# Transposing attention's probabilities on VectorE with transfers, in place of TensorE, in a float32 decoder step

## The chip, the cores and the metric

One core of a Trainium2 chip runs the whole program. The metric is the device time of one execution in microseconds, the median over runs. A core has five engines that run their own instruction lists in order and wait for each other by semaphores: TensorE (PE, with its weight loads PEld), VectorE (DVE), ScalarE (ACT), GpSimd (POOL) and SyncE (SP), which here only issues transfers.

## The reference, cut to what matters

A decoder step over a prompt of 1024 tokens and eight single-token samples: one pooling layer, a shared key and value projection, one attention layer. All in float32. What the change touches is the attention of the prompt:

```python
s = einsum('...qkgd,...skd->...kgqs', q, k) * (HEAD_DIM ** -0.5)
mask = (kp <= qp) & (qp - kp < WINDOW) & (kp >= 0)      # WINDOW = 128
s = where(mask, s, NEG)
m = maximum(max(s), sink)
p = exp(s - m)
p = p / (sum(p) + exp(sink - m))
o = einsum('...kgqs,...skd->...qkgd', p, v)
...
y = (o * silu(gate)) @ w_out
```

There are 32 query heads of 64 channels, 4 key and value heads, and blocks of 128 queries, each of which sees its own and the preceding block's keys. Since the window is exactly 128, a query sees exactly 128 keys of the 256: key place r of its own block if r is not after the query, else place r of the block before.

## The kernel before

The prompt is cut into two chunks of 512 tokens (chunk 1 carries the eight samples too, 520 columns), with channels on partitions. The large projections are done as sums and differences of quarters (units), each product in three float32r passes (L784, L785, L786: high by high, high by low, low by high). They are staged in four phases (`ai`, `ao` for the pooling layer, `bi`, `bo` for attention), each in three groups of units, A (chunk 0), C (mixed) and B (chunk 1). A unit is cut into ticks: a tick is one half of a unit, 24 products of 260 columns or 12 of 512. `self.i` counts the ticks.

Everything else is hung on ticks. `self.on(t, go, rank)` calls `go` after the matmuls of tick `t`, in the order of rank; `soft` tasks (weight casts, sums) are put where a cost count of the program finds VectorE or ScalarE free. TensorE, VectorE and ScalarE keep the order of the source; the queues of SP and GpSimd are ordered by the framework's scheduler. All tiles come from 53 slots of SBUF, the longest free slot first (`self.mem.full()`); a load waits until the slot's last reader is done.

Attention is done for a pair of heads at a time (`attend(c, t, at, meet)`, called "a head" below; 16 for each chunk, and "the last five heads" are those of chunk 1 from the twelfth on). `at` is the tick of its scores, and its steps hang on it:

- `at`: `score` (L1880) on TensorE into PSUM; `select` and `largest` choose the 128 visible scores of each query and take the maximum;
- `at+2`, `at+3`: `expo`; `at+4`, `at+5`: `norm` (L1928), on ScalarE: probabilities with 128 queries on partitions, 8 blocks of 128 keys side by side (4 blocks of queries, 2 heads);
- `at+6`: `turn`, eight TensorE transposes into PSUM (L1933), so that keys come to lie on partitions; `at+7`: `keep`, ScalarE's copy to SBUF (L1941), and `mask`, VectorE's product with a triangle (L1945);
- `at+meet`: `values`, the value products (L1962) in full float32, which the profile shows as two records for each product; a tick later `gate` on VectorE.

SP issues the loads of weights (`in_wib`, `in_wob`, and stored sums such as `sbi`), of activations, and RoPE's moves between partitions (`partner`, L1703, four transfers of 32 partitions). The decode of the samples (`decode`, from tick b+79 on) issues sixteen tiny moves there (L2069).

Of the kernel before, what the change touches and what calls it, by code (L numbers as in the profile page):

```python
# [16 lines left out]
P = 128  # L17
# [20 lines left out]
K_ID, K_MP, K_J, K_RC = 0, 128, 256, 384  # L38
# [122 lines left out]
class Kern:  # L161
# [1685 lines left out]
    def attend(self, c, t, at, meet=8):  # L1847


        nc = self.nc  # L1850
        T = CHUNKS[c][1]
        cst = self.cst
        S = lambda: self.S
        x = {}
# [70 lines left out]
        def norm(n):  # L1925
            rs = x["sm"][3]
            for i in range(4 * n, 4 * n + 4):
                nc.scalar.activation(x["s3"][:, i, :], x["s3"][:, i, :], AF.Copy, scale=rs[:, i : i + 1])  # L1928

        def turn():  # L1930
            PT = self.S[:, 0, :]
            for i in range(8):
                nc.tensor.transpose(  # L1933
                    PT[:, i * P : (i + 1) * P], x["sc"][:, i * P : (i + 1) * P], cst[:, K_ID : K_ID + P]
                )
            x["s"].free()

        def keep():
            PT = self.S[:, 0, :]
            x["w"] = self.mem.full()  # L1940
            nc.scalar.copy(x["w"].a[:, :1024], PT)  # L1941

        def mask():
            x["wp"] = self.mem.full()
            nc.vector.tensor_mul(  # L1945
                x["wp"].a[:, :1024].rearrange("p (i k) -> p i k", k=P),
                x["w"].a[:, :1024].rearrange("p (i k) -> p i k", k=P),
                cst[:, None, K_MP : K_MP + P].to_broadcast([P, 8, P]),
            )

        def values():
            o = x["o"] = self.psO()
            _, V, Vd = self.K[c]
            for b in range(NB):
                bs = slice(b * P, (b + 1) * P)
                parts = ((V[b + 1], x["w"].a), (Vd[b], x["wp"].a))
                parts = parts if c or b else parts[:1]
                for n, (v, p) in enumerate(parts):
                    for j in range(2):
                        vs = slice((2 * (t // 8) + j) * HD, (2 * (t // 8) + j + 1) * HD)  # L1960
                        ms = slice((2 * b + j) * P, (2 * b + j + 1) * P)
                        nc.tensor.matmul(  # L1962
                            o[64 * j : 64 * j + 64, bs], v[:, vs], p[:, ms], start=n == 0, stop=n == len(parts) - 1
                        )
            x["w"].free()
            x["wp"].free()
# [41 lines left out]
        self.on(at + 4, total, 3)  # L2008
        self.on(at + 4, lambda: norm(0))
        self.on(at + 5, lambda: norm(1))  # L2010
        self.on(at + 6, turn, 1)
        self.on(at + 7, keep, 3)
        self.on(at + 7, mask, 5)
        self.on(at + meet, values, 3)
        if c:
            self.on(at + 8, first)
# [159 lines left out]
    def attention(self):  # L2176
        a, c, b = (self.first["bi", g] for g in "ACB")
        self.on(a, lambda: self.kv_open(0), 0)
        self.on(b, lambda: self.kv_open(1), 0)
        for n in range(4):  # L2180
            for i in range(2):
                self.attend(0, 2 * n + i, a + 22 + 16 * n + 8 * i + (3 if n == 3 and i else 0))
                self.attend(0, 8 + 2 * n + i, c + 30 + 24 * n + 12 * i, 12 if n < 3 else 8)
        for n in range(4):
            for i, t in enumerate((8 + 2 * n, 9 + 2 * n, 2 * n, 2 * n + 1)):
                self.attend(1, t, b + 20 + 16 * n + 4 * i, 8 + (4 * n + i > 10))
        self.decode(b + 79)
        for c, n, t in ((0, 2, b + 7), (0, 2, b + 17), (1, 3, b + 81), (1, 3, b + 90)):
            self.on(t, lambda c=c, n=n: [self.kvs[c].pop(0).free() for _ in range(n)], 5)
        self.on(b + 72, lambda: self.rt.free(), 5)  # L2190

# [295 lines left out]
```

## Time and profile before

| | |
|---|---|
| median of 3 runs (lowest, highest) | 2274.58 us (2272.61 to 2276.1) |
| span of the profiled execution | 2272.0 us |
| busy: PE, PEld, DVE, ACT, POOL | 2262.4, 2130.5, 1598.4, 1136.1, 197.8 us |
| attention of chunk 0 (first and last transposes) | 1138 to 1676 us |
| attention of chunk 1 (first and last transposes) | 1722 to 1969 us |
| DMA | 556.43 MB, mean 245 GB/s |

The span is from the first to the last recorded instruction; the runs' times hold what lies around it too, and the profiled execution is one of its own, 2.6 us under the runs' median. A group's row gives line, engine, operation, out<-in, its count, busy us and mean ns of one, and the idle time ahead of it with what ended it. Records of matmuls overlap, so their mean is longer than the distance between two starts.

### The profile page before, as it was taken

The numbers are of one execution on the slowest core, as the hardware profiler recorded it, in microseconds if no ns is written. First come the engines' busy times: TensorE is split into PE (matmuls) and PEld (weight loads), VectorE is DVE, ScalarE is ACT, GpSimd is POOL, SyncE is SP. The second block draws the span as 40 slices with busy tenths as digits, with TensorE's granted clock in tenths as the row PEclk, the third lists the DMA queues.
The fourth block names the chain that finished last, engine by engine and source line by source line (L and its number), as shares of the span: only waits on it lengthen the run. The fifth ranks groups of instructions, "written<-read, shape, count | busy, mean of one in ns | idle before, by whom it ended". The sixth has DMA issues, their size and how long they took to land.

```text
span 2272.0 us, 42903 instructions
## 1 busy us (share of the span) xinstructions
PE 2262.4 (100%) x17312; PEld 2130.5 (94%) x17312; DVE 1598.4 (70%) x2009; ACT 1136.1 (50%) x2372; POOL 197.8 (9%) x418
## 2 busy tenths in 40 slices
PE   9999999999999999999999999999999999999998
PEld 7889999999999899999888899999999998889998
DVE  7667746746667587685786876666566879687688
ACT  6344333343334443454576644545647678553365
POOL 0101001100100111000011010101000000111000
PEclk9999999999999999999999999999999999999999
DMA  9859757673657898888488776666754556898873
GB/s 305 314 209 350 233 213 256 227 249 117 243 184 261 276 336 291 292 304 297 153 295 301 245 244 205 230 195 220 244 169 124 177 189 224 284 356 304 301 250 132
DMA packets 190262, 556.43 MB, mean 245 GB/s; under 512 B 26096, under 2 KB 31600, under 8 KB 190064
## 3 DMA queue, kind: packets, MB, share of 16 engines
q1 hardware_dynamic: 147936, 401.82, 54.0%
q0 software_dynamic: 41984, 151.61, 17.4%
q8 instruction: 135, 2.21, 0.4%
q14 instruction: 63, 0.52, 0.1%
q10 hardware_dynamic: 144, 0.27, 0.0%
HBM read 371.88 MB, written 171.16 MB: 239 GB/s over the span
## 4 chain that ended last, share of the span: by engine, by line
PE 96%; DVE 2%; ACT 1%; DMA 0%; issue 0%; SPq 0%; ACTq 0%; DVEq 0%
PE pD L784 28%; PE pD L786 28%; PE pD L785 28%; PE pD L1351 4%; PE pO L1962 2%; PE pS L1880 2%; PE pS L1933 1%; PE pD L848 1%; DVE m L619 0%; DMA m<-in_wia 0%; DVE m L407 0%; PE pO L848 0%; DMA m<-in_x 0%; PE pO L2087 0%; DVE m L1693 0%
## 5 line engine op out<-in xcount | busy, mean ns | idle before, releaser
L784 PE MATMUL pD<-m,m 128*128 128x260 f32 (+1 forms) x4736 | 1428.6, 302 | 0.4 <-ACT m L894 0.4
L786 PE MATMUL pD<-m,m 128*128 128x260 f32 (+1 forms) x4736 | 1420.7, 300 | 0.0
L785 PE MATMUL pD<-m,m 128*128 128x260 f32 (+1 forms) x4736 | 1420.2, 300 | 0.2 <-DVE m L619 0.2
L784 PEld LDWEIGHTS pD<-m,m 128*128 128x128 f32 x4736 | 891.7, 188 | 38.8 <-issue 5.5
L786 PEld LDWEIGHTS pD<-m,m 128*128 128x128 f32 x4736 | 891.4, 188 | 32.7
L785 PEld LDWEIGHTS pD<-m,m 128*128 128x128 f32 x4736 | 891.8, 188 | 31.9 <-DVE m L619 0.6
L407 DVE TENSOR_TENSOR m<-m,m 128x1024 fp32r<-128x1024 f32 x358 | 435.1, 1218 | 144.2 <-ACT m L399 118.9
L399 ACT CAST m<-m 128x1024 fp32r<-128x1024 f32 x358 | 373.0, 1045 | 48.4 <-DVE m L443 11.7
L443 DVE TENSOR_TENSOR m<-m,m 128x1024 f32<-128x1024 f32 x200 | 243.8, 1219 | 10.4 <-DMA m<-in_woa 2.5
L915 ACT COPY m<-pD 128x260 f32<-128x260 f32 (+1 forms) x126 | 56.0, 444 | 306.4 <-PE pD L786 306.0
L619 DVE TENSOR_TENSOR m<-m,m 128x1040 fp32r<-128x1040 f32 x108 | 130.0, 1234 | 24.1 <-ACT m L613 11.8
L924 ACT ACTIVATE m<-pD 128x260 f32<-128x260 f32 x100 | 38.7, 387 | 180.8 <-PE pD L786 172.7
L926 DVE TENSOR_TENSOR m<-pD,m 128x260 f32<-128x260 f32 x100 | 42.6, 426 | 113.0 <-PE pD L786 109.8
L613 ACT CAST m<-m 128x1040 fp32r<-128x1040 f32 x108 | 111.2, 1061 | 14.6 <-DVE m L407 6.7
L1915 ACT ACTIVATE m<-m,sm 128x128 f32<-128x128 f32 x256 | 99.2, 392 | 0.0
L1351 PE MATMUL pD<-m,m 128*128 128x260 f32 (+1 forms) x576 | 91.5, 319 | 0.0
L1351 PEld LDWEIGHTS pD<-m,m 128*128 128x128 f32 x576 | 82.0, 188 | 8.3
L896 ACT COPY m<-pD 128x260 f32<-128x260 f32 x68 | 25.6, 377 | 124.9 <-PE pD L786 124.9
L1945 DVE TENSOR_TENSOR m<-m,cst 128x1024 f32<-128x1024 f32 x32 | 39.1, 1221 | 69.0 <-ACT m L1941 68.7
L1928 ACT ACTIVATE m<-m,sm 128x128 f32<-128x128 f32 x256 | 81.8, 395 | 7.1 <-DVE sm L1923 7.1
L881 ACT ACTIVATE m<-pD 128x512 f32<-128x512 f32 x50 | 29.8, 597 | 99.4 <-PE pD L786 90.6
L894 ACT ACTIVATE m<-pD 128x260 f32<-128x260 f32 x68 | 26.4, 388 | 101.3 <-PE pD L786 101.3
(246 smaller groups left out, 1857.1 us busy)
## 6 DMA issues: line engine op xcount, KB each, us to landing
m<-in_wib SPq DMA_DIRECT2D x96, 512.0 KB, 5.0
m<-in_wia SPq DMA_DIRECT2D x94, 512.0 KB, 5.6
m<-in_woa SPq DMA_DIRECT2D x48, 512.0 KB, 6.2
m<-in_wob SPq DMA_DIRECT2D x48, 512.0 KB, 7.0
sbi<-m POOLq DMA_DIRECT2D x36, 512.0 KB, 4.2
m<-sbi SPq DMA_DIRECT2D x36, 512.0 KB, 4.5
m<-in_x SPq DMA_DIRECT2D x32, 520.0 KB, 7.4
sai<-m POOLq DMA_DIRECT2D x32, 512.0 KB, 3.9
```

The source lines that it names most:

```text
L399: self.nc.scalar.copy(e["hi"].r[:, :1024], e["raw"].a[:, :1024])
L407: self.nc.vector.tensor_sub(o.r[:, :1024], s.a[:, :1024], e["hi"].a[:, :1024])
L443: self.nc.vector.tensor_add(s[o].a[:, :1024], s[a].a[:, :1024], s[b].a[:, :1024])
L613: self.nc.scalar.copy(h.r[:, : 2 * TMAX], s.a[:, : 2 * TMAX])
L619: self.nc.vector.tensor_sub(o.r[:, : 2 * TMAX], s.a[:, : 2 * TMAX], h.a[:, : 2 * TMAX])
L784: nc.tensor.matmul(ps[:, :w], wh[:, s], h, start=new and n2 == 0, stop=False, skip_group_check=on)
L785: nc.tensor.matmul(ps[:, :w], wh[:, s], l, start=False, stop=False, skip_group_check=on)
L786: nc.tensor.matmul(ps[:, :w], wl[:, s], h, start=False, stop=n2 == 7, skip_group_check=on)
L915: self.evac(ph, pos)(self.dest(ph, pos, m, 0)(cs), ps[:, : cs.stop - cs.start])
L1351: nc.tensor.matmul(ps[:, : cs.stop - cs.start], ws[:, s], d[:, cs], start=f0 and k == 0, stop=l0 and k == 3,)
L1915: nc.scalar.activation(x["s3"][:, i, :], x["s3"][:, i, :], AF.Exp, bias=nm[:, i : i + 1], scale=0.125, accum_out=rs[:, i : i + 1],)
L1928: nc.scalar.activation(x["s3"][:, i, :], x["s3"][:, i, :], AF.Copy, scale=rs[:, i : i + 1])
```

## The change

`turn` becomes one VectorE instruction: it transposes each 32x32 block of the probabilities where it stands, within its 32 partitions. A new step, `move`, then brings the blocks to the partitions on which their keys belong, by 16 transfers from SBUF to SBUF on SP's queue (32 partitions, 1 KB each). `keep` is gone. The moved tile has another order of columns (4 quarters of queries, 8 blocks, 32 queries), and `mask` and the value products read it so (`quarter`): the value product's moving operand is four runs of 32 columns. The value products come later: `meet` goes from 8 to 16 (heads 1 to 5) or 11 (heads 6 to 8) in group A of chunk 0, stays at 12 for the first six heads of group C and goes from 8 to 12 and 14 for its last two, and goes from 8 to 12 for the first eleven heads of chunk 1; the last five keep 9. `mask` stands one tick ahead of `values`. Chunk 0's keys and values are freed 5 ticks later.

```diff
         def turn():
-            PT = self.S[:, 0, :]
-            for i in range(8):
-                nc.tensor.transpose(
-                    PT[:, i * P : (i + 1) * P], x["sc"][:, i * P : (i + 1) * P], cst[:, K_ID : K_ID + P]
-                )
+            X = x["t"] = self.mem.full()
+            nc.vector.transpose(
+                X.a[:, :1024].rearrange("p (j t r) -> p t j r", j=4, t=8),
+                x["sc"][:, :1024].rearrange("p (t j r) -> p t j r", j=4, t=8),
+            )
             x["s"].free()
 
-        def keep():
-            PT = self.S[:, 0, :]
-            x["w"] = self.mem.full()
-            nc.scalar.copy(x["w"].a[:, :1024], PT)
+        def move():
+            W, X = self.mem.full(), x.pop("t")
+            x["w"] = W
+            for i in range(4):
+                for j in range(4):
+                    nc.sync.dma_start(
+                        W.a[32 * j : 32 * j + 32, 256 * i : 256 * i + 256],
+                        X.a[32 * i : 32 * i + 32, 256 * j : 256 * j + 256],
+                    )
+            X.free(True)
+
+        def quarter(a):
+            return a[:, :1024].rearrange("p (i t r) -> p i t r", i=4, t=8)
 ...
-                            o[64 * j : 64 * j + 64, bs], v[:, vs], p[:, ms], start=n == 0, stop=n == len(parts) - 1
+                            o[64 * j : 64 * j + 64, bs], v[:, vs], quarter(p)[:, :, 2 * b + j, :],
+                            start=n == 0, stop=n == len(parts) - 1,
 ...
-        self.on(at + 6, turn, 1)
-        self.on(at + 7, keep, 3)
-        self.on(at + 7, mask, 5)
+        self.on(at + 6, turn, 2)
+        self.on(at + (6 if meet < 10 else 7), move, 3)
+        self.on(at + meet - 1, mask, 5)
         self.on(at + meet, values, 3)
 ...
-                self.attend(1, t, b + 20 + 16 * n + 4 * i, 8 + (4 * n + i > 10))
+                self.attend(1, t, b + 20 + 16 * n + 4 * i, 9 if 4 * n + i > 10 else 12)
 ...
-        for c, n, t in ((0, 2, b + 7), (0, 2, b + 17), (1, 3, b + 81), (1, 3, b + 90)):
+        for c, n, t in ((0, 2, b + 7), (0, 2, b + 22), (1, 3, b + 81), (1, 3, b + 90)):
```

Where the instructions stand. On TensorE, in group B before, at the transposes of the twelfth head of chunk 1 (pS is the attention's PSUM tile, pD a projection's, m a slot):

```order
L786 MATMUL pD_20912<-m_1709_17585,m_1935_20840 128x260
L1933 MATMUL pS_11329<-cst,m_1933_20827 128x128 x8
L784 MATMUL pD_20961<-m_1702_17540,m_1929_20752 128x260
L785 MATMUL pD_20961<-m_1706_17579,m_1929_20752 128x260
L786 MATMUL pD_20961<-m_1702_17540,m_1935_20840 128x260
```

The same kind of place in the change, behind the value products of an earlier head; no row of transposes is left:

```order
L1969 MATMUL pO_21245<-m_1965_21182,m_1726_17740 64x128 x2
L1969 MATMUL pO_21245<-m_1945_20923,m_1727_17741 64x128 x2
L784 MATMUL pD_21158<-m_1700_17542,m_1938_20849 128x260
L785 MATMUL pD_21158<-m_1705_17582,m_1938_20849 128x260
L786 MATMUL pD_21158<-m_1700_17542,m_1953_21037 128x260
```

On VectorE before, around the mask of that head (L1945; L926 evacuates projections, L407 is a weight's low part, L1900 the score selection of the head after the next):

```order
L926 TENSOR_TENSOR m_1939_20910<-pD_20961,m_1921_20701 128x260
L1945 TENSOR_TENSOR m_1966_21208<-m_1965_21202,cst 128x1024
L1922 TENSOR_TENSOR sm_21097<-sm_21097,sm_21096 128x8
L1923 RECIPROCAL sm_21097<-sm_21097 128x8
L407 TENSOR_TENSOR m_1974_21265<-m_1938_20884,m_1949_21064 128x1024
L1900 COPY_PREDICATED m_1971_21255<-mki,pS_11329 128x1024
```

And in the change: the transpose (L1932), and further down the masks (L1954) of the head before and of this head, the second of which reads the moved tile m_1981:

```order
L926 TENSOR_TENSOR m_1959_21116<-pD_21118,m_1941_20887 128x260
L1932 STREAM_TRANSPOSE m_1980_21357<-m_1951_21024 128x8x4x32
...
L926 TENSOR_TENSOR m_1959_21116<-pD_21158,m_1941_20887 128x260
L1954 TENSOR_TENSOR m_1987_21426<-m_1964_21161,cst 128x1024
L1922 TENSOR_TENSOR sm_21305<-sm_21305,sm_21304 128x8
L1923 RECIPROCAL sm_21305<-sm_21305 128x8
L1954 TENSOR_TENSOR m_1995_21500<-m_1981_21360,cst 128x1024
L407 TENSOR_TENSOR m_1997_21504<-m_1955_21079,m_1989_21430 128x1024
L1900 COPY_PREDICATED m_1993_21492<-mki,pS_11329 128x1024
```

VectorE has one instruction more for each head, and its mask now waits for transfers instead of ScalarE's copy, with the next weight's low part and the next head's selection behind it. On SP's queue before, at the decode's tiny moves (L2069, in_cv the cached values):

```order
L384 DMA m_2018_21696<-in_wob 128x1024
L2063 DMA m_2016_21692<-in_cv 128x1024
L2069 DMA m_2017_21693<-m_1716_17618 1x16x8
L603 DMA m_2020_21701<-to 128x2x512
L2069 DMA m_2016_21692<-m_1716_17618 1x16x8
L603 DMA m_2022_21734<-to 128x2x512
L2069 DMA m_2016_21692<-m_1716_17618 1x16x8 x7
L2069 DMA m_2017_21693<-m_1716_17618 1x16x8 x4
```

And in the change, where the decode's moves are L2077 and a head's moves L1943 (the last head but one, then the last):

```order
L1943 DMA m_2049_21984<-m_2047_21979 32x256 x16
L384 DMA m_2052_22032<-in_wob 128x1024
L2077 DMA m_2043_21958<-m_1728_17742 1x16x8 x8
L2077 DMA m_2044_21959<-m_1728_17742 1x16x8 x4
L2080 DMA out_nvs<-m_2043_21958 128x1024
L2077 DMA m_2044_21959<-m_1728_17742 1x16x8 x4
L384 DMA m_2057_22121<-in_wob 128x1024
L1943 DMA m_2059_22138<-m_2058_22135 32x256
L2080 DMA out_nvs<-m_2044_21959 128x1024
L1943 DMA m_2059_22138<-m_2058_22135 32x256 x15
```

Sixteen issues a head are new on this queue, and between those of the last two heads stand the sixteen of the decode and four whole tiles.

More of the change, by code (lines that the diff above doesn't have):

```diff
@@ L1945, in mask @@
             nc.vector.tensor_mul(
-                x["wp"].a[:, :1024].rearrange("p (i k) -> p i k", k=P),
-                x["w"].a[:, :1024].rearrange("p (i k) -> p i k", k=P),
-                cst[:, None, K_MP : K_MP + P].to_broadcast([P, 8, P]),
+                quarter(x["wp"].a), quarter(x["w"].a),
+                cst[:, K_MP : K_MP + P].rearrange("p (i r) -> p i r", i=4)[:, :, None, :].to_broadcast([P, 4, 8, 32]),
             )
@@ L1960, in values @@
                         vs = slice((2 * (t // 8) + j) * HD, (2 * (t // 8) + j + 1) * HD)
-                        ms = slice((2 * b + j) * P, (2 * b + j + 1) * P)
                         nc.tensor.matmul(
-                            o[64 * j : 64 * j + 64, bs], v[:, vs], p[:, ms], start=n == 0, stop=n == len(parts) - 1
+                            o[64 * j : 64 * j + 64, bs], v[:, vs], quarter(p)[:, :, 2 * b + j, :],
+                            start=n == 0, stop=n == len(parts) - 1,
                         )
@@ L2179, in attention @@
         self.on(b, lambda: self.kv_open(1), 0)
[L2180 to L2183, printed above, removed]
+        at = [22, 30, 38, 46, 54, 62, 70, 81]
+        for n, (t, meet) in enumerate(zip(at, (16, 16, 16, 16, 16, 11, 11, 11))):
+            self.attend(0, n, a + t, meet)
+        for n in range(8):
+            self.attend(0, 8 + n, c + 30 + 12 * n, 12 if n < 7 else 14)
         for n in range(4):
             for i, t in enumerate((8 + 2 * n, 9 + 2 * n, 2 * n, 2 * n + 1)):
-                self.attend(1, t, b + 20 + 16 * n + 4 * i, 8 + (4 * n + i > 10))
+                self.attend(1, t, b + 20 + 16 * n + 4 * i, 9 if 4 * n + i > 10 else 12)
         self.decode(b + 79)
-        for c, n, t in ((0, 2, b + 7), (0, 2, b + 17), (1, 3, b + 81), (1, 3, b + 90)):
+        for c, n, t in ((0, 2, b + 7), (0, 2, b + 22), (1, 3, b + 81), (1, 3, b + 90)):
             self.on(t, lambda c=c, n=n: [self.kvs[c].pop(0).free() for _ in range(n)], 5)
```

## The prediction

> **What bounds the kernel now.** I read the page first: the busy shares and the chain of work that ended last.
>
> ```profile
> PE 2262.4 (100%) x17312; PEld 2130.5 (94%) x17312; DVE 1598.4 (70%) x2009; ACT 1136.1 (50%) x2372; POOL 197.8 (9%) x418
> PE 96%; DVE 2%; ACT 1%; DMA 0%; issue 0%; SPq 0%; ACTq 0%; DVEq 0%
> ```
>
> TensorE is busy all the time and is 96% of the chain: a microsecond less on TensorE is a microsecond less in all, and a microsecond in which TensorE waits is one more. Every other engine is cover. So I need two sums: what leaves TensorE, and where TensorE will now wait.
>
> **What leaves TensorE.** The groups by line (form kept apart; busy us, mean ns) and the timeline of TensorE around one batch of transposes (start, length):
>
> ```profile
> L1933 PE MATMUL pS<-cst,m 128*128 128x128 f32 x256 | 33.3, 273 | 0.0
> L1962 PE MATMUL pO<-m,m 128*64 128x128 f32 x960 | 59.5, 276 | 0.3 <-DVE m L2108 0.3
> ...
> 1299.23 0.28 PE L786 MATMUL pD<-m,m 128*128 128x260 f32 x1
> 1299.35 1.04 PE L1933 MATMUL pS<-cst,m 128*128 128x128 f32 x8
> 1300.15 0.36 PE L784 MATMUL pD<-m,m 128*128 128x260 f32 x1
> 1300.35 0.28 PE L785 MATMUL pD<-m,m 128*128 128x260 f32 x1
> 1300.47 0.28 PE L786 MATMUL pD<-m,m 128*128 128x260 f32 x1
> ```
>
> Matmul records overlap, so I price by starts. Projections start every 0.12 us. The batch takes 1299.35 to 1300.15 = 0.80, and the projection behind it waits 0.20 instead of 0.12 for its successor: 0.88 us a head. 32 heads: **-28.2 us**. The group's busy time (33.3) would count the overlap twice.
>
> The value products stay, 960 records. Their moving operand becomes four runs of 32 columns instead of one of 128. No row shows such an operand: the bounds are 0 and one more of the same, 59.5 us. I take 0: a record costs 59.5/960 = 62 ns, two (the halves j) 124 ns, in which a projection streams 260 columns, so 128 columns leave room.
>
> **What is added off TensorE.** The rows nearest to VectorE's transpose (1024 elements a partition) are these, and the second is the mask that stays:
>
> ```profile
> L1900 DVE COPY_PREDICATED m<-mki,pS 128x1024 f32<-128x1024 int32 x32 | 42.5, 1330 | 19.4 <-issue 15.4 <-ACT m L1896 3.9
> L1945 DVE TENSOR_TENSOR m<-m,cst 128x1024 f32<-128x1024 f32 x32 | 39.1, 1221 | 69.0 <-ACT m L1941 68.7 <-issue 0.3
> ```
>
> I take 1.25 us, between them (bounds 1.2 and, for an operation twice as slow, 2.5): 32 x 1.25 = 40 us more for VectorE, which is 70% busy. ScalarE loses 32 copies. Both are covered on average; where not, below. By "VectorE: DVE Perf Modes" of the Trainium skill (The three transpose paths: 311 ns for 128x128 in bf16) eight blocks would be 2.5 us, an estimate, which no run here shows; by it the sum below would be some 5 us higher.
>
> The new cost sits on SP's queue. Sixteen transfers SBUF to SBUF a head are issued one after the other. The same kind, by line: RoPE's (L1703) and the decode's (L2069), with the time from issue to landing, and eleven of them in a row:
>
> ```profile
> L1703 SPq DMA_DIRECT2D m<-m x80: 507/588/2155, 1072.0 to 1873.5; - x80
> DMA to landing us min/median/max: 2.0/4.2/8.9
> ...
> L2069 SPq DMA_DIRECT2D m<-m x16: 502/587/1566, 1940.3 to 1957.8; - x16
> DMA to landing us min/median/max: 1.7/2.9/4.6
> ...
> 1950.62 7.81 SPq L2069 DMA_DIRECT2D m<-m  x11
> ```
>
> One holds SP for 0.59 us whether it moves 128 KB or 32 bytes a partition, and about 0.64 with the step to the next; eleven took 7.81, 0.71 each. Sixteen are 16 x 0.64 = 10.2 us (11.4 by the other figure). So the path from normalized probabilities to the first value product becomes: transpose 1.25, issues 10.2, landing of the last 2.9, mask 1.22: **15.6 us** (14.7 with the shortest landing, 17 with the slow issue). The old path, transposes, copy, mask, was some 3 us.
>
> **Where the window is long enough.** The value products of chunk 0 come 5 to 10 ticks after the transpose, a tick being at least 24 x 0.12 = 2.9 us of TensorE: 14.5 us and another head's scores at the shortest. Here I put 1 us for three heads with 5 ticks. For the first eleven heads of chunk 1 a head comes every
>
> ```profile
> 1738.55 1.03 PE L1933 MATMUL pS<-cst,m 128*128 128x128 f32 x8
> 1754.66 1.03 PE L1933 MATMUL pS<-cst,m 128*128 128x128 f32 x8
> ```
>
> 16.1 us, 15.2 without its transposes. SP needs 10.2 of that, and two of RoPE's transfers and about three loads a head (some 1.3 + 1.1): 12.6, so the queue keeps up, at 83%. The window there is six ticks (17) and the products of other heads between, about 21 us: no wait. The transfers' bytes, 32 x 16 x 32 KB = 17 MB, lie in the cover of a DMA share of about a half in that stretch.
>
> **Where it is not.** The last five heads keep their value products three ticks behind the transpose. For each, the end of its normalization on ScalarE and the start of its value products on TensorE, from the timelines (start, length):
>
> ```profile
> 1897.10 1.27 ACT L1928 ACTIVATE m<-m,sm 128x128 f32<-128x128 f32 x4
> 1910.66 1.97 PE L1962 MATMUL pO<-m,m 128*64 128x128 f32 x32
> 1914.05 1.27 ACT L1928 ACTIVATE m<-m,sm 128x128 f32<-128x128 f32 x4
> 1926.88 1.31 PE L1962 MATMUL pO<-m,m 128*64 128x128 f32 x20
> 1928.68 1.29 ACT L1928 ACTIVATE m<-m,sm 128x128 f32<-128x128 f32 x4
> 1948.40 1.97 PE L1962 MATMUL pO<-m,m 128*64 128x128 f32 x32
> 1949.07 1.28 ACT L1928 ACTIVATE m<-m,sm 128x128 f32<-128x128 f32 x4
> 1963.07 1.17 PE L1962 MATMUL pO<-m,m 128*64 128x128 f32 x17 [0.29 <-DVE m L2108]
> 1966.21 1.27 ACT L1928 ACTIVATE m<-m,sm 128x128 f32<-128x128 f32 x4
> 1977.38 1.86 PE L1962 MATMUL pO<-m,m 128*64 128x128 f32 x30
> ```
>
> The windows are 12.3, 11.6, 18.4, 12.7 and 9.9 us; the head's own transposes leave them, so 11.4, 10.7, 17.5, 11.8, 9.0. Against 15.6 TensorE waits 4.2, 4.9, 0, 3.8 and 6.6. The last head has more ahead of it: in the order, all sixteen tiny transfers of the decode and four others stand between its moves and those of the head before. SP then has 1.25 + 10.2 + 16 x 0.71 + 4 x 0.35 = 24.2 us from the one normalization to the next move, and 1967.48 - 1950.35 - 0.88 + 3.8 + 1.25 = 21.3 us are there: 3 us more. Together **+22.5 us** (17 with the short landing and a turn that starts early, 32 with the slow issue). Each wait is VectorE's too: the mask that waits for the moves stands ahead of the next heads' L1900 and of weight differences (L407). That costs nothing twice, since TensorE stands still in the same time, but the stretch has no slack:
>
> ```profile
> 1900.00:1930.00 30.00, 29.92 (x226) 24.66 (x225) 29.61 (x40) 27.36 (x72) 1.75 (x4) 1.00 0.74 264
> ```
>
> The columns are the stretch, then busy time of PE, PEld, DVE, ACT and POOL, then clock, DMA share and GB/s. VectorE is busy for 29.61 of 30 us, so two transposes of 1.25 add **+2.5** (0 to 5). Loads are queued behind moves: in the order, several weights now stand only a few rows ahead of their cast. The later products also hold a head's tiles 4 to 8 ticks longer, of 53 slots that the loads need too. What waits is an engine with slack of a few us; no row prices it, the bounds are 0 and half a us for each of some twenty such loads, and I take **+3** (0 to 10).
>
> **The clock.** A wait also costs afterwards. The decode's thin matmuls are followed by a stretch at half speed:
>
> ```profile
> 1935.34 3.64 PE L2087 MATMUL pO<-qd,m 128*128 128x16 f32 x32
> ...
> 1939.15 0.46 PE L785 MATMUL pD<-m,m 128*128 128x512 f32 x1
> ...
> 1942.39 0.57 PE L784 MATMUL pD<-m,m 128*128 128x512 f32 x1
> 1942.79 0.40 PE L785 MATMUL pD<-m,m 128*128 128x512 f32 x1
> 1943.03 0.40 PE L786 MATMUL pD<-m,m 128*128 128x512 f32 x1
> ...
> 1938.80:1942.40 3.60, 3.60 (x12) 2.84 (x12) 2.08 (x6) 0.71 (x1) 0.00 (x0) 0.58 0.98 381
> ```
>
> The granted clock is 0.58 there. From 1939.15 to 1942.79, 3.64 us, nine matmuls of 512 columns start, where the last two starts shown are 0.24 apart: 9 x 0.24 = 2.2, so about 1.5 us lost, after 3.5 us of little work. I count three such losses, **+4.5** (0 to 8). "TensorE: Matmul & The Clock Gate" of the Trainium skill (Part 1) has a free-running window of about 3.4 us that has to be idle. By it only a wait over 6.8 us is sure to hold a whole one, and the sum would have one loss, 3 us less; the row above, which is not an idle window, speaks for the shorter wait.
>
> **The sum.** -28.2 + 1 + 22.5 + 2.5 + 3 + 4.5 = +5.3 us on a profiled span of 2272.0. The median of the runs, 2274.58, lies 2.6 above that span, so about 2279.9; I say **2280**.
>
> **Rivals.**
> - *The waits stay under the gain* (faster). For it: nothing is moved by TensorE any more, and moves could start before SP reaches them by my reckoning, since in the trace normalization ends up to 2.8 us ahead of the old transposes. It decides when the four short heads wait less than 28.2 in all, clock included: with 17 for them and 1.5 for the last one's clock, -28.2 + 18.5 = -10, 2265. Against it: 10.2 us of issue in a window of 9 to 12. Chance 0.23.
> - *SP becomes the bound of all of chunk 1.* At 0.71 us the moves are 11.4 of 15.2, the queue 14 of 15.2; any wait of SP for a slot or a landing then adds up, and the loads behind it are late for ScalarE. For it: RoPE's transfers took up to 2155 ns; against it: the median. If half of eleven heads wait 2 us more and the last five take the slow issue: +5.3 + 10 + 8 = +23, 2298. Chance 0.19.
> - *An operation is dearer*: the transpose at 2.5 us adds 1.25 to four windows (+5, 2285), the strided value operand up to 59.5 (2339). Chance 0.08 in all, most of it for the first.
>
> **How the numbers follow.** The forecast has 0.50: waits at the end about equal to the gain, or a little more, 2270 to 2291. The range holds it, the faster rival's and the second's time: 2262 to 2302; beyond it lie the strided operand and parts of both rivals. A difference of 0.2%, 4.5 us, is about what a measurement here can tell from none. Faster by that much: the rival's 0.20 and 0.02 of the forecast, 0.22. Within: 0.27, from the forecast's lower half. Slower: the rest, 0.51.
>
> **What would show it.** Right: no row of L1933; TensorE idle by some 25 us within the last five heads, ended by VectorE's mask or shown at the value products, and none to speak of earlier; SP with groups of sixteen of about 10 us; half clock behind the longest waits. Wrong: sixteen issues in clearly under 10 us; value products of the last heads without a wait; TensorE waiting for ScalarE or VectorE in the first heads of chunk 1 or in chunk 0 (slots and loads, not moves); value-product records well above 62 ns each.

## The result and the profile after

The kernel after takes 2365.42 us, median of 4 runs (2359.86 to 2368.03), beside 2273.86 for the kernel before: a ratio of 1.0399, interval 1.0384 to 1.0413. It is slower by 91.6 us; the forecast was +5.3 and its range ended at 2302. In the profiled executions the span is 2358.0 against 2272.0, 86.0 more.

The busy shares and the chain of work that ended last, of the kernel after:

```profile
PE 2264.4 (96%) x17056; PEld 2124.9 (90%) x17056; DVE 1637.1 (69%) x2041; ACT 1107.8 (47%) x2340; POOL 198.1 (8%) x418
PE 75%; DMA 8%; SPq 7%; DVE 6%; ACT 2%; issue 2%; DVEq 0%; ACTq 0%
```

TensorE was 100% busy and 96% of the chain; now DMA, SP's queue and VectorE hold 21% of it. The 256 transposes are gone, and TensorE waits instead. Where, the windows say (stretch, length, then busy time of PE, PEld, DVE, ACT and POOL, granted clock, DMA share, GB/s):

```profile
1100.00:1200.00 100.00, 97.70 (x528) 78.56 (x526) 77.90 (x99) 65.04 (x138) 12.41 (x31) 1.00 0.71 247
1200.00:1300.00 100.00, 86.71 (x473) 69.91 (x470) 68.92 (x85) 50.08 (x119) 12.01 (x28) 0.95 0.79 265
1300.00:1400.00 100.00, 97.69 (x849) 96.09 (x847) 69.42 (x77) 47.54 (x118) 9.27 (x19) 0.98 0.67 233
...
1800.00:1900.00 100.00, 88.45 (x840) 85.13 (x840) 74.46 (x116) 63.49 (x197) 5.42 (x8) 0.93 0.62 194
1900.00:2000.00 100.00, 78.86 (x615) 70.67 (x614) 71.97 (x104) 57.41 (x163) 5.98 (x12) 0.88 0.64 202
...
1100.00:1900.00 800.00, 754.13 (x6098) 705.89 (x6096) 561.31 (x719) 432.13 (x1129) 66.36 (x138) 0.98 0.66 219
1900.00:2070.00 170.00, 133.72 (x994) 115.04 (x993) 106.14 (x158) 82.52 (x227) 13.55 (x29) 0.89 0.64 210
```

TensorE stands still for 36.3 us of the last stretch (170.00 - 133.72), which holds the value products of the last five heads. It stands still for 45.9 us (800.00 - 754.13) *before* it, where I had forecast next to nothing; in the kernel before it stands still for 0.8 us of the same 1100 to 1900. The waits by engine and line, first TensorE's of 1900 to 2070, then TensorE's of 1100 to 1900, then of the whole span those of VectorE and ScalarE that feed it, and SP's (waiting line, releaser: us in all, times, longest):

```profile
PE pO L1969 <- DMA m<-m: 13.9, 2, 11.4
PE pS L1880 <- ACT m L1859: 9.7, 1, 9.7
PE pO L1969 <- DVE m L1954: 5.1, 4, 3.1
PE pO L1969 <- DVE m L1984: 4.2, 1, 4.2
PE pO L1969 <- issue: 2.9, 1, 2.9
...
PE pS L1880 <- DVE m L1863: 16.9, 9, 6.0
PE pD L784 <- ACT pD L977: 12.1, 3, 7.0
PE pD L784 <- ACT m L881: 6.3, 4, 2.8
PE pO L1807 <- ACT m L924: 4.7, 1, 4.7
...
DVE m L1709 <- DMA m<-m: 56.6, 11, 9.7
DVE m L1954 <- DMA m<-m: 44.2, 7, 14.9
DVE m L443 <- DMA m<-in_wib: 33.3, 8, 7.3
ACT m L399 <- DMA m<-sbi: 35.2, 8, 9.8
ACT m L1859 <- DVE m L1932: 10.9, 1, 10.9
SPq L1943 <- DVE m L1932: 68.6, 19, 12.4
```

L1969, the value products, wait 13.9 + 5.1 + 4.2 + 2.9 = 26.1 us at the end: the waits I had forecast. The other rows are of another kind. From 1100 to 1900 TensorE waits for the queries' rest that VectorE computes (L1863) and for ScalarE's copies between PSUM and SBUF (L977, L881, L924). These engines wait for transfers in their turn: L1709 is the first of RoPE's three instructions on VectorE; it overwrites the tile that RoPE's transfers (L1703) read, so it waits for them. L443 and L399 wait for weights. None of these transfers is a head's move (only L1954, the mask, waits for those); SP issues them all, between the moves. The row of L1709 must not be taken whole: it was 9.6 us before, but it is 15.3 to 27.7 in the runs below without moves (runs 2, 4 and 8), and its longest wait here, 9.7, comes at 1078 us, ahead of the first move.

The timeline of the kernel after shows the chain once, SP's queue, then VectorE, ScalarE and TensorE:

```profile
1655.80 11.21 SPq L1943 DMA_DIRECT2D m<-m  x16
1667.11 4.96 SPq L1703 DMA_DIRECT2D m<-m  x8
...
1671.06 0.70 DVE L1709 TENSOR_TENSOR m<-m,m 128x520 f32<-128x520 f32 x1 [6.93 <-DMA m<-m]
1671.67 0.69 DVE L1710 TENSOR_TENSOR m<-m,m 128x520 f32<-128x520 f32 x1
1672.40 0.70 DVE L1711 TENSOR_TENSOR m<-m,m 128x520 f32<-128x520 f32 x1
...
1673.19 0.62 ACT L1763 CAST m<-m 128x512 fp32r<-128x512 f32 x1 [5.72 <-DVE m L1711]
1673.72 0.38 ACT L924 ACTIVATE m<-pD 128x260 f32<-128x260 f32 x1
...
1674.15 0.47 PE L1807 MATMUL pO<-cst,m 128*128 128x128 f32 x1 [4.73 <-ACT m L924]
```

Sixteen moves hold SP for 11.21 us. RoPE's transfers get out right behind them, from 1667.11 on, and VectorE stands 6.93 us for them. ScalarE's cast of the keys (L1763) waits for RoPE's sum (L1711), and the copy out of PSUM behind it in ScalarE's order (L924) is what TensorE waits 4.73 us for. Each engine works in order, so the late transfer delays everything behind its reader. Not every wait of L1709 is so plain: one of 9.42 us, up to 1280.98, comes behind moves too, but its transfers were issued by 1272.76 and took another 8 us to land, where the median from issue to landing is 3.8.

### The profile page after: what moved, and what is told of

Its sections match the earlier page's. It is cut to its first block, busy times and chain, and to the rows that moved or that the text cites. A ratio compares the mean times of both kernels' runs of the same rounds, so it can differ in the third digit from the quotient of the medians.

```text
span 2358.0 us, 43224 instructions
## 1 busy us (share of the span) xinstructions
PE 2264.4 (96%) x17056; PEld 2124.9 (90%) x17056; DVE 1637.1 (69%) x2041; ACT 1107.8 (47%) x2340; POOL 198.1 (8%) x418
## 4 chain that ended last, share of the span: by engine, by line
PE 75%; DMA 8%; SPq 7%; DVE 6%; ACT 2%; issue 2%; DVEq 0%; ACTq 0%
PE pD L784 22%; PE pD L785 22%; PE pD L786 22%; SPq L1943 5%; PE pD L1351 4%; DMA m<-m 2%; DMA m<-in_wib 2%; PE pS L1880 2%; PE pO L1969 1%; PE pD L848 1%; DMA m<-to 1%; DMA m<-sbi 1%; SPq L1703 1%; DVE m L407 1%; DVE m L619 1%
## 5 line engine op out<-in xcount | busy, mean ns | idle before, releaser
L407 DVE TENSOR_TENSOR m<-m,m 128x1024 fp32r<-128x1024 f32 x358 | 435.3, 1218 | 149.7 <-ACT m L399 119.9
L399 ACT CAST m<-m 128x1024 fp32r<-128x1024 f32 x358 | 372.8, 1045 | 135.5 <-DMA m<-sbi 35.2
L443 DVE TENSOR_TENSOR m<-m,m 128x1024 f32<-128x1024 f32 x200 | 244.0, 1220 | 45.1 <-DMA m<-in_wib 33.3
L924 ACT ACTIVATE m<-pD 128x260 f32<-128x260 f32 x100 | 38.6, 386 | 169.8 <-PE pD L786 161.6
L926 DVE TENSOR_TENSOR m<-pD,m 128x260 f32<-128x260 f32 x100 | 42.6, 426 | 97.9 <-PE pD L786 86.4
L1969 PE MATMUL pO<-m,m 128*64 128x128 f32 x960 | 69.5, 303 | 27.2 <-DMA m<-m 13.9
L1969 PEld LDWEIGHTS pO<-m,m 128*64 128x64 f32 x960 | 60.5, 154 | 34.3 <-issue 19.0
L1880 PE MATMUL pS<-m,m 64*128 64x256 f32 x768 | 60.3, 301 | 28.1 <-DVE m L1863 17.5
L1880 PEld LDWEIGHTS pS<-m,m 64*128 64x128 f32 x768 | 51.1, 196 | 37.6 <-DVE m L1863 20.0
```

Source lines behind the costliest of these rows:

```text
L399: self.nc.scalar.copy(e["hi"].r[:, :1024], e["raw"].a[:, :1024])
L407: self.nc.vector.tensor_sub(o.r[:, :1024], s.a[:, :1024], e["hi"].a[:, :1024])
L443: self.nc.vector.tensor_add(s[o].a[:, :1024], s[a].a[:, :1024], s[b].a[:, :1024])
L1880: nc.tensor.matmul(self.S[:, j, o : o + 256], q[r, b * P : (b + 1) * P], win(k, i)[r], start=n == 0, stop=n == 2,)
L1969: nc.tensor.matmul(o[64 * j : 64 * j + 64, bs], v[:, vs], quarter(p)[:, :, 2 * b + j, :], start=n == 0, stop=n == len(parts) - 1,)
```

## The experiments

Times are medians in us; each ratio is to the kernel before on the same chip, with its 95% interval. The theory after the first look at the result: groups of sixteen on SP's in-order queue make RoPE's transfers and the loads late. Rivals: the later value products and the tiles they hold; VectorE's transposes; the bytes; the strided operand. A `...` in an edit stands for lines left out.

**1. The moves on GpSimd's queue.**

```diff
-                    nc.sync.dma_start(
+                    nc.gpsimd.dma_start(
                         W.a[32 * j : 32 * j + 32, 256 * i : 256 * i + 256],
```

> The kernel after the change, its sixteen moves a head issued by GpSimd instead of SP; nothing else is changed. Theory (SP's queue works in order: while it issues moves, or stands before them waiting for VectorE's transpose, RoPE's transfers and the weight loads behind are late): most of VectorE's wait for RoPE's transfers (56.6 us) and of ScalarE's and VectorE's waits for weights go, the scores' waits with them, and only the five last heads' waits for their own moves stay: 2285 to 2320. Rival one (the later value products hold tiles longer, and VectorE's transposes crowd its queue; the queue of SP is a bystander): 2350 to 2370 as before the edit. Rival two (the bytes of the moves slow all transfers): no change either, 2350 to 2370, with landings as long as now.

Measured: 2317.75, ratio 1.019 (1.0175 to 1.0206). 47.7 us came back, with bytes and schedule as they were. Part of what is left moved to GpSimd's queue, which works in order too: a memset that the selection of chunk 0's heads needs (L1894) now stands behind moves, and VectorE waits for it, which it didn't before. The 27.2 us for RoPE's transfers are no more than in run 8, which has no moves at all (27.7).

```profile
DVE m L1709 <- DMA m<-m: 27.2, 9, 8.4
DVE m L1900 <- POOL m L1894: 22.2, 5, 7.0
```

**2. No moves.** The tile that VectorE has turned in blocks is used as it is; values are taken with wrong keys.

```diff
-            W, X = self.mem.full(), x.pop("t")
-            x["w"] = W
-            for i in range(4):
...
-            X.free(True)
+            x["w"] = x.pop("t")
```

> The kernel after the change without its sixteen moves a head: mask and value products read VectorE's block-transposed tile as it is (left out: the movement between partitions, so the values are of wrong keys). VectorE's transposes, the later value products and their strided operand all stay. Theory (the moves alone cost the time): the whole 28 us come out, 2240 to 2255. Rival one (later value products and crowded VectorE): 2300 to 2330. Rival three (the strided operand of the value products costs TensorE): 10 to 60 us above the theory, with value products' starts further apart.

Measured: 2270.78, ratio 0.9981 (0.9971 to 0.999). A miss for the theory in its strict form: the moves are 95 of the loss (91.6 + 3.7), but without them only 3.7 of some 28 us come out. The strided operand is cleared: the value products of the same head and length, before (L1962) and here (L1961), and the first and last of six batches of chunk 0, before and here:

```profile
1746.90 1.97 PE L1962 MATMUL pO<-m,m 128*64 128x128 f32 x32
1420.94 1.75 PE L1962 MATMUL pO<-m,m 128*64 128x128 f32 x28
...
1615.36 1.75 PE L1962 MATMUL pO<-m,m 128*64 128x128 f32 x28
```

```profile
1748.03 1.97 PE L1961 MATMUL pO<-m,m 128*64 128x128 f32 x32
1414.43 1.75 PE L1961 MATMUL pO<-m,m 128*64 128x128 f32 x28
...
1604.60 1.75 PE L1961 MATMUL pO<-m,m 128*64 128x128 f32 x28
```

1.97 and 1.75 either way. From head to head it is (1615.36 - 1420.94) / 5 = 38.88 before and (1604.60 - 1414.43) / 5 = 38.03 here: 0.85 us a head are really gone from TensorE, 27.2 for 32 heads if all are worth the same.

**3 and 4. The kernel before with sixteen extra moves a head on SP (nobody reads them), and with the changed schedule alone.**

```diff
+        def extra():
+            W, X = self.mem.full(), x["w"]
+            for i in range(4):
+                for j in range(4):
+                    nc.sync.dma_start(W.a[32 * j : 32 * j + 32, 256 * i : 256 * i + 256],
+                                      X.a[32 * i : 32 * i + 32, 256 * j : 256 * j + 256])
+            W.free(True)
...
+        self.on(at + 7, extra, 3)
```

> The kernel before the change (TensorE transposes, value products at their old place), with sixteen extra moves a head on SP, of the same sizes, from the copied probabilities into a spare tile that nobody reads. No value product waits for a move here. Theory (SP's queue in order makes RoPE's transfers and loads late): 2310 to 2340, with VectorE waiting for RoPE's transfers and ScalarE for loads. Rival one (later products, VectorE): 2274 to 2280.

> The kernel before the change with the changed schedule alone: mask and value products at the later places of the changed kernel, tiles held as long as there; transposes stay on TensorE, there are no moves. Theory (SP's queue): 2272 to 2282. Rival one (the later products' tiles and order): 2310 to 2340.

Measured: 2396.2, ratio 1.0534 (1.0519 to 1.055), and 2279.24, ratio 1.0024 (1.0014 to 1.0033). Moves that nobody waits for cost 121.7 us, more than the whole change, and nearly twice the most that was expected (2340 is 66 more): the mechanism is the expected one, its size was not. The later value products and the tiles they hold cost 4.8, as expected. VectorE's wait for RoPE's transfers in the kernel with extra moves, and a wait for weights:

```profile
DVE m L1709 <- DMA m<-m: 60.7, 12, 8.8
ACT m L399 <- DMA m<-in_wob: 29.3, 4, 14.2
```

**5 and 6. Issues or bytes.** In place of sixteen moves four of all 128 partitions by 256 columns (same bytes), or sixteen of 8 columns in place of 256. The edit of the four, against the `extra` of run 3:

```diff
-                    nc.sync.dma_start(W.a[32 * j : 32 * j + 32, 256 * i : 256 * i + 256], ...
+                nc.sync.dma_start(W.a[:, 256 * i : 256 * i + 256], X.a[:, 256 * i : 256 * i + 256])
```

> The kernel before the change with four extra moves a head on SP in place of sixteen: all 128 partitions by 256 columns each, so the same bytes in a quarter of the issues. With sixteen it took 121.7 us more. Theory (what costs is the time that SP's queue gives to issues, 16 x 0.59 us a head): a quarter or less, 2276 to 2305. Rival (the bytes through the DMA engines, 512 KB read and written a head): as with sixteen, 2370 to 2400.

> The kernel before the change with sixteen extra moves a head on SP, of 32 partitions by 8 columns: 32 bytes a partition in place of 1 KB, a thirty-second of the bytes in the same issues. Theory (issues): 2370 to 2400, as with the full moves. Rival (bytes): 2274 to 2285. If an issue is cheaper for a small transfer, between the two, by the mean duration of an issue.

Measured: four wide ones 2286.11, ratio 1.0052 (1.0039 to 1.0066), +11.8; sixteen tiny ones 2383.57, ratio 1.0481 (1.0465 to 1.0497), +109.2. A thirty-second of the bytes takes a tenth off the cost; a quarter of the issues takes nine tenths off. So it isn't the bytes. SP's issue durations, min/median/max in ns, of the wide and the tiny:

```profile
L1946 SPq DMA_DIRECT2D m<-m x128: 470/599/1854, 1143.8 to 1986.7; - x128
...
L1947 SPq DMA_DIRECT2D m<-m x512: 507/589/1973, 1144.1 to 2087.8; - x171
```

One more rival is settled by these traces. SP also stands still in front of moves until another engine releases them (68.6 us in the kernel after, for L1932), and holds up all that stands behind in that time too. In front of the extra moves it does so about as long, for ScalarE, with sixteen in a row (run 3) as with four wide ones (run 5):

```profile
SPq L1947 <- ACT m L1915: 39.8, 14, 6.8
...
SPq L1946 <- ACT m L1915: 50.1, 15, 6.3
```

The second kernel pays 11.8 us in all, so there this wait is not what costs.

**7. Only the nineteen heads with long windows are turned by VectorE, moves on GpSimd; the other thirteen as before.**

```diff
+        if vec:
+            self.on(at + 6, turn, 2)
+            self.on(at + 7, move, 3)
+            self.on(at + meet - 1, mask, 5)
+        else:
+            self.on(at + 6, turn_pe, 1)
+            self.on(at + 7, keep, 3)
+            self.on(at + 7, mask, 5)
 ...
```

> Only the nineteen heads with long windows are turned by VectorE (the last eight of chunk 0, the first eleven of chunk 1), with their moves on GpSimd's queue; the first eight of chunk 0 and the last five of chunk 1 keep TensorE's transposes and their old places. Theory (the loss of the first run with GpSimd's queue, +43 us, sits at the heads taken out: memsets behind moves in chunk 0, short windows at the end; between 1330 and 1890 us its TensorE had gaps of 6 us in all): 19 x 0.86 = -16 us against before, with up to 8 us of waits left: 2258 to 2268. Rival (VectorE's order, crowded by the transposes, costs time there too): 2272 to 2285.

Measured: 2273.19, ratio 0.9995 (0.9986 to 1.0004). The rival: no gain. It goes at one place above all, `PE pS L1880 <- ACT m L1859`, 5.4 us in one wait at 1875, with 6.8 us of half clock behind it; how the rest of the 16 us expected goes was not separated.

**8. No moves, and ScalarE copies in place of VectorE's transposes** (probabilities untransposed).

```diff
-            nc.vector.transpose(
-                X.a[:, :1024].rearrange("p (j t r) -> p t j r", j=4, t=8),
-                x["sc"][:, :1024].rearrange("p (t j r) -> p t j r", j=4, t=8),
-            )
+            nc.scalar.copy(X.a[:, :1024], x["sc"][:, :1024])
 ...
```

> The kernel after the change without moves, and VectorE's 32 transposes replaced by 32 plain copies on ScalarE of the same 1024 columns (left out: the transposition; masks and value products read untransposed probabilities). VectorE has its old load, TensorE has no transposes, the schedule is the changed one. Theory (the 20 us by which the run without moves stayed above -28 + 4.7 come from VectorE's 40 us of transposes, which make the queries' rests, masks and weight differences late where VectorE is near full): 2248 to 2260. Rival (the shorter heads leave every engine too little time, whoever turns): 2265 to 2275 as with VectorE.

Measured: 2253.15, ratio 0.9909 (0.9895 to 0.9922), within the theory's range. So to have the transposes on VectorE and not on ScalarE costs about 17.6 us (2270.78 - 2253.15), by medians; the two profiled spans, 2267.1 and 2257.3, show 9.8 of it. The largest piece in the run without moves is a chain, not a full VectorE (VectorE, ScalarE, TensorE):

```profile
1870.44 0.43 DVE L926 TENSOR_TENSOR m<-pD,m 128x260 f32<-128x260 f32 x1 [7.83 <-DMA to<-m]
1870.78 1.24 DVE L1932 STREAM_TRANSPOSE m<-m 128x1024 f32<-128x1024 f32 x1
...
1872.05 0.62 ACT L1859 CAST m<-m 128x512 fp32r<-128x512 f32 x1 [8.72 <-DVE m L1932]
...
1872.72 0.75 PE L1880 MATMUL pS<-m,m 64*128 64x256 f32 x4 [4.33 <-ACT m L1859]
```

VectorE stands 7.83 us for a tile that a store still reads. The transpose stands behind that, and the cast of a later head's queries (L1859) behind the transpose, because it takes over the tile that the transpose frees. TensorE used to read and free that tile. The kernel after has the same chain, with a wait of 10.9 us for L1932 (row above); TensorE's 9.7 us for L1859 between 1900 and 2070 are its end, so some of that belongs to the transposes and not to the moves (4.3 here, without any move). Run 8 has neither VectorE's wait for the store nor ScalarE's for the transpose; what makes the store's wait go with VectorE's transposes stays open. That is one piece; how the rest of the 17.6 is spread wasn't separated.

**9. The extra moves of the third run in four groups of four, one a tick.**

```diff
-        self.on(at + 7, extra, 3)
+        for i in range(4):
+            self.on(at + 7 + i, lambda i=i: extra(i), 3)
 ...
```

> The kernel before the change with the same sixteen extra moves a head on SP, full size, but in four groups of four over four ticks instead of sixteen in a row. In a row they took 121.7 us more; SP issues some 1.2 us in 2 even then (per 100 us of the worst stretch 76 us of issues), so its mean load has room. Theory (a transfer that stands behind a whole group comes up to 10 us late, and its reader has less slack than that; what costs is the length of the group, not SP's load): groups of four hold the queue for 2.5 us, and most of the loss goes: 2280 to 2320. Rival (SP's load in sum, each issue making all that follows later): 2360 to 2400, as in a row.

Measured: 2308.5, ratio 1.0147 (1.0133 to 1.0161): +32.7 in place of +121.7, with issues and bytes unchanged. So most of the cost, 89.0 us, is the length of the group and not SP's load in sum. The four wide moves of run 5, a quarter of the issues, cost 11.8; how much of the 32.7 is load wasn't separated.

**10 and 11. Seven and thirteen heads on VectorE and GpSimd**, with the edit of the seventh run (`vec` true for the last eight of chunk 0 but one, and for none or the first six of chunk 1).

> Only seven heads, the last of chunk 0 but one, are turned by VectorE, with moves on GpSimd's queue; all others as before the change, at their old places. Theory (with nineteen the gain of 16 us was eaten by VectorE between 1870 and 1910 us and by the later products of the last head of chunk 0; in this stretch of chunk 0 VectorE has 28% free): 7 x 0.86 = -6.0, 2267 to 2270. Rival (transposes cost time on VectorE wherever they stand): 2273 to 2277.

> The seven heads and the first six of chunk 1 are turned by VectorE, with moves on GpSimd's queue; all others as before the change, at their old places. Theory (VectorE has 22 to 32% free up to about 1760 us, and what comes late there is made up before 1870): 13 x 0.86 = -11, 2262 to 2266. Rival (what VectorE falls behind in chunk 1 stays with it until the end, where it is full): 2268 to 2278, with TensorE's waits for the queries' rests between 1860 and 1910 us.

Measured: 2274.15, ratio 0.9992 (0.9983 to 1.0000), and 2278.05, ratio 1.0013 (1.0004 to 1.0022). Both missed. With thirteen, one wait of value products for VectorE's gate (L2004) took 6.8 us at 1820. With seven, the seventh head's value products stood four ticks later than before, behind the turn of chunk 1's values; run 13 leaves just this head out and is faster by 3.9 us.

**12. The kernel after with the moves of 27 heads in four groups of four**, still on SP; the last five heads as they were.

```diff
-        self.on(at + (6 if meet < 10 else 7), move, 3)
+        if meet < 10:
+            self.on(at + 6, move, 3)
+        else:
+            for i in range(4):
+                self.on(at + (7 if meet > 11 else 6) + i, lambda i=i: move((i,)), 3)
 ...
```

> The kernel after the change, with the moves of the 27 heads whose value products come eleven ticks or more behind their scores' tick issued in four groups of four, one group a tick, still all on SP; the last five heads of chunk 1 keep their sixteen in a row. Same issues, same bytes. Theory (groups of sixteen make RoPE's transfers and loads late by up to the group's length): the waits of TensorE before the last five heads (some 55 us with the clock behind them) mostly go, the last five heads' own (some 35 to 40 with the clock) stay: 2300 to 2330, VectorE's wait for RoPE's transfers well under the 56.6 us of now. Rival (SP's load in sum): 2350 to 2370.

Measured: 2330.05, ratio 1.0246 (1.0229 to 1.0263), at the edge of what was expected: 35.4 us came back.

```profile
DVE m L1709 <- DMA m<-m: 31.3, 11, 9.2
PE pO L1971 <- DMA m<-m: 18.0, 6, 8.3
PE pO L1971 <- DVE m L1956: 9.8, 10, 4.4
```

The value products (L1971) now wait longer in all than in the kernel after (18.0 for transfers in place of 13.9, 9.8 for the mask in place of 5.1), so some of the gain is given back; that the last tick's group is what they wait for is likely, but not shown.

**13 and 14. Six heads whose value products already stood twelve ticks behind**, nothing else changed: moves on GpSimd's queue, and on SP's.

> Six heads, the first six of the last eight of chunk 0, whose value products stood twelve ticks behind their scores' tick already before the change: VectorE turns them, GpSimd's queue moves them, and nothing else of the kernel before is changed, no place in the order either. Theory (with seven heads TensorE was 5.4 us ahead after six of them, and lost it where the seventh's value products, then four ticks later than before, stood behind the turn of chunk 1's values: 1.2 + 1.4 + 0.6 us near 1650, and 2.4 us and a half-speed stretch at 1902): 2274 - 5.2 = 2269, or 2272 if the wait at 1902 stays. Rival (each head taken off TensorE is given back by the engines around, wherever it stands): 2273 to 2276.

> The same six heads with their moves on SP's queue, sixteen in a row. Theory (a group of sixteen makes what stands behind it on SP late): in the changed kernel each of these heads' scores came 0.7 to 2.0 us late, so about 6 x 1.3 = 8 us more than on GpSimd's queue, 2275 to 2281. Rival (in this stretch a head comes only every 38 us and SP has room): as on GpSimd's queue, within 2 us.

Measured: 2270.28, ratio 0.9975 (0.9965 to 0.9985), and 2274.3, ratio 0.9995 (0.9986 to 1.0003). The first beats both kernels, the one before by 5.4 us where 6 x 0.86 = 5.2 were expected: a head taken off TensorE is worth its price where nothing else gets late. On SP's queue the same six give most of it back, 4.0 us, even with a head only every 38 us; that is half of the 8 us expected, and lies just under the range given. VectorE in that run, its waits for these weights in all, and TensorE's waits:

```profile
1418.88 1.23 DVE L443 TENSOR_TENSOR m<-m,m 128x1024 f32<-128x1024 f32 x1 [7.24 <-DMA m<-in_wib]
...
DVE m L443 <- DMA m<-in_wib: 27.4, 6, 7.2
...
PE pS L1880 <- DVE m L1863: 4.3, 6, 1.0
```

A weight comes late behind the group, six times, and the scores of each of the six heads wait up to 1.0 us.

## Why the prediction was wrong

The direction was right, with a chance of 0.51; the size was out by 86 us, and most of it came from a mechanism that the forecast had priced at next to nothing. By its own steps:

- *-28.2 for TensorE's transposes*: right, 27.2 by the head spacing.
- *0 for the strided operand*: right. The end at 59.5 can be dropped.
- *VectorE's transpose 1.25*: right, and the estimate of 2.5 from the Trainium skill ("VectorE: DVE Perf Modes", The three transpose paths) doesn't hold here:

```profile
L1932 DVE STREAM_TRANSPOSE m<-m x32: 1233/1238/1247, 1138.6 to 2032.1; 128x1024 f32<-128x1024 f32 x32
```

- *0.64 us an issue and 10.2 for sixteen*: right in size, 0.59 each and 10.55 in the group above.
- *+22.5 for the last five heads*: right in mechanism and nearly in size, 26.1. The last head's wait is 11.4 (the longest in the row of L1969 and DMA), forecast at 6.6 + 3.
- *"so the queue keeps up, at 83%", and no wait before the last five heads*: this step failed. TensorE stood still for 45.9 us there. SP had time to spare: the durations of its issues add up to 57 of the 100 us from 1700 and 68 of those from 1800. The value products of these heads didn't wait for their moves either. Others did: the transfers behind a group. What decides is how long one transfer stands behind a group (some 10 us) against the slack of its reader. Runs 9 and 12 changed that length, with the same issues and bytes, and gave 89.0 and 35.4 us back. The second rival came nearest ("the loads behind it are late for ScalarE", at 0.19), but it had them late because SP's load fills its time, and priced them at 2 us each for half of eleven heads.
- *+3 for loads queued behind moves (0 to 10)*: the term of the sum that was mis-sized. "Half a us for each of some twenty such loads" had no row behind it. Run 3 puts sixteen moves a head, without any reader, at 121.7, and leaving the moves out gives back 95 us (run 2), of which about 26 are the waits at the end.
- *+2.5 for VectorE*: 17.6 by runs 2 and 8. I counted its busy time in one stretch and not what takes its tiles.
- *+1 for chunk 0's later products*: run 4 puts all the later products, with the tiles they hold, at 4.8.
- *+4.5 for the clock*: 26 to 29. TensorE's busy time rose by 2.0 us (2264.4 against 2262.4) though 27.2 us of work had left it, so the same work took 29.2 us longer. The trace of the kernel after has 14 stretches at half clock before its end, 71.7 us together; TensorE is busy for 52.0 us of them, and half of that, 26.0, is the most they can have cost. By the window rule of the Trainium skill ("TensorE: Matmul & The Clock Gate", Part 1) I had weighed one loss, and three by a row; both were far too few, mostly because there were many more waits than forecast.

By medians the parts close: -27.2 for the transposes, +17.6 for VectorE, +95.3 for the moves (2365.42 - 2273.86 + 3.71), and 5.9 are left for the schedule, which run 4 put at 4.8. Of the 95.3, 35.4 go when the groups of 27 heads are cut in four, and about 26.1 are the forecast waits at the end; how the rest divides between the clock and the shorter groups' waits stays open.

Of the signs named ahead, four came out for it (no L1933, SP's groups of about 10 us, waits at the last value products, half clock behind the longest waits). The one that was to show it wrong did: TensorE waiting for ScalarE and VectorE in the first heads. The cause named there, "slots and loads, not moves", was only half of it: it was the loads, and RoPE's transfers, behind the moves.

## What to carry to other kernels

A queue that works in order is judged by its longest block against the slack of what stands behind it, not by its load in the mean: spread a burst over ticks, or give it a queue on which nothing urgent waits. What a small transfer costs its queue is the issue, so count issues before bytes. Time taken off the bounding engine is only kept where every tile and transfer around it still has slack: move the easiest cases first and look, here six heads of thirty-two.

## What the hardware showed

- An issue costs SP the same 589 ns for 32 bytes and for 1 KB a partition, and 599 for four times the partitions (medians of runs 6, 3 and 5). GpSimd took 498 for the same move (run 1):

```profile
L1943 POOL DMA_DIRECT2D m<-m x512: 498/498/532, 1140.5 to 2005.5; - x171
```

  "DMA: Bandwidth & Descriptors" of the Trainium skill (Rules for kernel authors) says that spreading transfers over issuing engines doesn't help bandwidth and only saves issue time. Run 1 agrees on the issue time, and here that was worth 47.7 us; that the bandwidth isn't helped, no run here tests.
- Half clock follows many waits that are shorter than its shortest stretch, 3.4 us. Over the sixteen traces, counted where TensorE stood still for over 0.5 us after 1000 us: of 39 waits of 4 us and more all 39 were followed by half clock (a stretch that began between the wait's start and 3.4 us after its end), 12 of 13 of 3 to 4 us, 16 of 24 of 2 to 3, 11 of 55 of 1 to 2, 5 of 51 below. The stretches, but for the one at each trace's end, lasted 3.4, 6.8, 10.2 or 13.7 us. "TensorE: Matmul & The Clock Gate" of the Trainium skill (Part 1) has a free-running window of about 3.4 us, and half clock after an idle one; the lengths agree with that, but a wait of 2 to 3 us can't fill a window, and 16 of 24 were followed by half clock all the same. So the window need not be wholly idle here; where the limit lies, these traces don't show.
- A strided moving operand of four runs of 32 fp32 columns streams like one run of 128 (1.97 us for 32 either way).
